# Low key parts of the attention scores on 64 rows of TensorE, two heads in turn, and the first scores among the values

## The chip, the core and the metric

The kernel runs on one core of a Trainium2 chip, in one launch. The metric is the device time of that launch in microseconds (us). Below, PE is the matrix engine (TensorE), PEld its weight loads, DVE VectorE, ACT ScalarE, POOL GpSimd, SP the engine that issues the transfers (DMA).

## What is computed

A decoder trunk of two layers on 256 positions of width 1024: a recurrent block with a squared-ReLU MLP, then sparse attention with a squared-ReLU MLP, each behind an RMS norm, and a last norm. The change touches the attention, of which this is the core (with 256 positions every block is selected and the window holds all earlier positions, so the selected and the window branch are plain causal attention with keys of their own):

```python
for each query block of 128 and each group of 4 heads:
    s_c = q.k_c - slope*d    # 15 compressed keys
    s_s = q.k_s - slope*d    # "selected" keys
    s_w = q.k_w - slope*d    # "window" keys
    o   = g0*softmax(s_c).v_c + g1*softmax(s_s).v_s + g2*softmax(s_w).v_w
```

There are 16 heads of 64 dimensions in 4 groups; a group shares its keys and values.

## The kernel before, in words

All of the large products are made in three passes of a reduced-precision float (fp32r): an operand x is split into a high part and a low part (x minus the high part), and PE adds high times high, high times low and low times high into one PSUM bank (`mm3`, L317 to L320). Weights come by DMA in pieces of 128 by 1024, ACT or DVE writes the high part (L326), DVE the low part (L323), in the order of `weight_pieces`. PE's program therefore is a long row of matmuls of 256 columns, lines L318, L319 and L320.

The attention section is recorded as tasks (`add`) with an engine, an assumed duration, what they read and write, and a due time. `Plan.emit` then lays the tasks out with these durations and a random seed (`SEEDS`), and the instructions of each engine are written in that order. Nothing is reordered on the chip afterwards: each engine works through its own row and waits on semaphores.

The steps of the section:

- `cproj` and `kchunk` (0, 0 and 0, 1) make the compressed inputs and the keys of the first two groups; `hidden` (L955), `kc_out` (L965) and `vc_out` (L984) make the compressed keys and values. `hidden` and the later `pv` (L1162) address 64 columns of PE's array at a time, two such halves in turn; `kc_out` and `vc_out` address 64 rows; every other matmul uses all 128 rows and 128 columns.
- `values` (L1005 to L1007) makes values and gates: 8 steps over the width, each with four matmul triples into four banks, and 96 matmuls in all.
- `qchunk(c)` makes the queries of two heads that lie in two groups. Its result sits in two tiles: `sa[c]` holds the high part of the first head's query in rows 0 to 63 and its low part in rows 64 to 127; `sb[c]` holds the second head's, high in rows 64 to 127, low in rows 0 to 63. The low parts get into the other rows by DMA (`move`).
- `kchunk(gp, br)` makes keys for two groups. `kh` has the high part of each group's keys twice, in both halves of the rows (the second copy by DMA); `kl` has the low part in the group's own rows, by DMA, and zeros in the other 64 rows (a POOL memset, L869).
- `scores(s)`: one head in three parts: both branches for the first 128 queries (288 columns with the compressed keys), the window or the selected branch for the last 128 queries (272 columns) and the other one (256 columns). Each part is two matmuls into one of three banks (2, 3, 4 in turn): L1098 with `kh` (all 128 rows, high and low query times high key) and L1099 with `kl` (all 128 rows, of which 64 of `kl` are zero). DVE then takes the bank (L1109 adds the distance term and takes the row's extreme, L1116 the same for the compressed keys, each followed by a short read of the accumulator), ACT takes the exponential (L1112).
- `rescale` (DVE, ACT), `transposes` (six on PE, L1147) and `pv` (probabilities times values, L1162) follow for each head or pair of heads. Probabilities lie in `pts`, of which there are NPT = 3, by head in turn.
- The fillers: between the parts of the scores PE does the remaining projections (`fillers`) and the first half of the output projection (`out_t`), all of them rows of L318 to L320.

The order before: `values` right after the compressed keys, then `qchunk(0)`, and the first scores at a due time of 37; the stages of the heads are TSTAGE = 5 apart.

Of the kernel before, what the change touches and what calls it, by code (L numbers as in the profile page):

```python
# [15 lines left out]
OP = mybir.AluOpType  # L16
# [15 lines left out]
NPT, NTL = 3, 3  # L32
TSTAGE, FPS = 5.0, 3.25
CST = (3.5, 7.5, 11.5, 15.2)
SEEDS, ROUNDS, SHIFT = (64, 5), 6, 1.5
# [16 lines left out]
def weight_pieces():  # L52

    order = []
    order += [{"c": ("in", 8 + i), "y": ("in", i)}[k] for k, i in RG_ORDER if k != "g"]
    order += [("out", m) for m in range(8)]
    order += mlp_pieces(0)
    order += [("ck", 0), ("ck", 1), ("cv", 0), ("cv", 1), ("ks", 0), ("kw", 0)]
    order += [("v", i) for i in range(4)]
    order += [("q", m) for m in range(4)]  # L60
    order += [("ks", 1), ("kw", 1)]
    order += [("q", m) for m in range(4, 8)]
    order += [("o0", m) for m in range(4)]
    order += [("o1", m) for m in range(4)]
    order += mlp_pieces(1)
    return order
# [153 lines left out]
def trunk_kernel(ctx: ExitStack, tc: tile.TileContext, x_in, vec_in, const_in, w2_in, wts, out):  # L220
# [607 lines left out]
    with ExitStack() as ph:  # L828
# [17 lines left out]
        kh, kl = (at.tile([P, 4 * GK + NCP], F32R, name=n) for n in ("kh", "kl"))  # L846
        kpair = lambda y, g, n: y[:, g * GK:g * GK + 2 * (S + NCP)].rearrange("p (b k) -> p b k", b=2)[:, :, :n]
        kcomp = lambda y: y[:, :4 * GK].rearrange("p (g k) -> p g k", g=4)[:, :, P:PC]
# [20 lines left out]
        add("pool", 1.74, lambda e: e.memset(kl.bitcast(F32), 0.0), w=["kl"], t=-9)  # L869
# [27 lines left out]
        def kchunk(gp, br, b, t, step):  # L897
            z, zk = proj_t(("ks", "kw")[br], gp, b, t, step)
            t += 4 * step
            x, xk, l_, lk = turn()  # L900
            add("dve", 0.34, lambda e: e.tensor_tensor(x, z(), rs, op=OP.mult), r=[zk, "rs"], w=[xk], t=t)
            x, l_ = two_blocks(x), two_blocks(l_)
            for hf in range(2):
                g = gp * 2 + hf
                add(HI, copy(kset(kh, g, br), x), r=[xk], w=[("k", g, br), ("k", g, br, 1)], t=t + 0.5)
            add("dve", 0.34, diff(l_, x, kset(kh, gp * 2, br)), r=[xk, ("k", gp * 2, br), ("k", gp * 2, br, 1)], w=[lk], t=t + 1)
            for hf in range(2):
                own, oth, g = own_(hf), own_(1 - hf), gp * 2 + hf
                move(kset(kh, g, br)[oth], kset(kh, g, br)[own], [("k", g, br)], [("k", g, br, 1)], t + 0.8)
                move(kset(kl, g, br)[own], l_[own], [lk, "kl"], [("k", g, br, 2)], t + 1.2)  # L910

        def kkeys(g, br):
            return [("k", g, br), ("k", g, br, 1), ("k", g, br, 2)]
# [49 lines left out]
        def kc_out(t):  # L963
# [4 lines left out]
            add("act", 0.1, lambda e: e.copy(kcomp(kh), o4()), r=[("ps", 6)], w=["kch"], t=t)  # L968
            for hf in range(2):
                own = own_(hf)  # L970
                add("dve", 0.15, lambda e, own=own, hf=hf: e.tensor_tensor(
                    kcomp(kl)[own, hf::2], o4()[own, hf::2], kcomp(kh)[own, hf::2].bitcast(F32), op=OP.subtract),
                    r=[("ps", 6), "kch", "kl"], w=[("kcl", hf)], t=t)
# [17 lines left out]
        def values(t):  # L991
            banks = ((2, 3), (4, 5))
            ncol = (S + 48, S)
            vz = [[zview(("v", h, b), banks[h][b], lambda x, b=b: x[:, :ncol[b]]) for b in range(2)] for h in range(2)]
            for i in range(4):
                wh, wl, wk = weight("v", i, t + 2.8 * i)
                for kk in range(2):
                    k = 2 * i + kk
                    for h in range(2):
                        def run(e, wh=wh, wl=wl, k=k, kk=kk, h=h):  # L1000
# [8 lines left out]
                            t=t + 2.8 * i + 1.4 * kk + 0.7 * h)  # L1009
            t += 11.2  # L1010
# [64 lines left out]
        def scores(s, t):  # L1075
            p, c, hf = heads[s]
            g = 2 * p + hf
            slope = float(2.0 ** (-8.0 * (g * 4 + c + 1) / 16))
            cc = (4 * p + c) % NQ
            x, xk = (sb, sa)[1 - hf][cc], ("sb" if hf else "sa", cc)  # L1080
            xk = [xk, xk + (1,)]
            mx, sm, pt = mxs[s % 4], sms[s % 4], pts[s % NPT]
            a, cj = s // 4, s % 4
            cview = lambda y, n, k: y[:, :2 * n].rearrange("p (b k) -> p b k", b=2)[:, :, :k]
            parts = ((0, lambda x: cview(x, PC, PC), lambda y: kpair(y, g, PC), (0, 1), 0.26),
                     (1, lambda x: x[:, :S + NCP], lambda y: y[:, g * GK:g * GK + S + NCP], (0,), 0.25),
                     (1, lambda x: x[:, :S], lambda y: y[:, g * GK + S + NCP:(g + 1) * GK], (1,), 0.23))
            for i, (qc, view, keys_, sets, d) in enumerate(parts):
                nk = (qc + 1) * P
                n = sn["n"]  # L1090
                sn["n"] += 1
                b = sbank[n % 3]
                bk = [("ps", b)]
                z = zview(("s", s, i), b, lambda x: x)

                def run(e, z=z, qc=qc, view=view, keys_=keys_):
                    qs = slice(qc * P, (qc + 1) * P)
                    e.matmul(view(z()), x[:, qs], keys_(kh), start=True, stop=False)  # L1098
                    e.matmul(view(z()), x[:, qs], keys_(kl), start=False, stop=True)  # L1099
                add("pe", d, run, r=xk + ["kl", "kch", ("kcl", 0), ("kcl", 1)] + kkeys(g, 0) + kkeys(g, 1), w=bk, t=t)  # L1100
                for b in sets:
                    o, j = qc * 2 * P + b * nk, 2 * qc + b
                    mk, pk = ("mx", s % 4, j), ("pt", s % NPT, qc, b)
                    row = pt[:, o:o + nk]
                    dist = cst[:, C_D0 + qc * P:C_D0 + qc * P + nk]
                    src = (lambda z, b=b: cview(z(), PC, P)[:, b]) if qc == 0 else (
                        (lambda z: z()[:, :S]) if b else lambda z: cview(z(), PC, P))
                    shape = two_blocks if (qc, b) == (1, 0) else lambda y: y
                    add("dve", (0.2, 0.34)[qc], lambda e, z=z, src=src, shape=shape, dist=dist, row=row, j=j: e.tensor_tensor_reduce(  # L1109
                        shape(row), src(z), shape(dist), -slope, -NEG, OP.add, OP.min, mx[:, j:j + 1]),  # L1110
                        r=bk + ["cst"], w=[mk, pk], t=t + 0.3)
                    add("act", (0.39, 0.49)[qc], lambda e, row=row, j=j: e.activation(  # L1112
                        row, row, AF.Exp, bias=mx[:, j:j + 1], scale=-1.0, accum_out=sm[:, j:j + 1]), r=[mk, "tab"],
                        w=[pk, ("sm", s % 4, j)], t=t + 0.6)
                if 0 in sets:
                    add("dve", 0.22, lambda e, z=z, qc=qc: e.tensor_tensor_reduce(  # L1116
                        css[a % 2][:, cj, qc], z()[:, P:PC], cst[:, C_DC + qc * NCP:C_DC + (qc + 1) * NCP], -slope, -NEG, OP.add,
                        OP.min, cmx[a % 2][:, 2 * cj + qc:2 * cj + qc + 1]),
                        r=bk + ["cst", ("sq", 0), ("sq", 1)], w=[("cs", a % 2), ("cm", a % 2)], t=t + 0.35)
# [91 lines left out]
        table(AF.Exp, 24)  # L1211
        values(20.5)
        gate_t(34)
        qchunk(0, 6, 34, PJ)
        T0, T = 37.0, TSTAGE
        fillers = [("q", c) for c in (1, 2, 3)] + [("ks", 1), ("kw", 1)] + [("q", c) for c in (4, 5, 6, 7)]
        step = T / FPS
        events = []
        for i, (nm, c) in enumerate(fillers):
            t = T0 + 4 * i * step  # L1220
# [4 lines left out]
        for m in range(8):  # L1225
            t = T0 + (n0 + 2 * m) * step
            events.append((t, 0, lambda m=m, t=t: out_t(0, m, (len(fillers) + m) % 2, t, step)))
        for s in range(16):
            events.append((T0 + s * T, 1, lambda s=s: scores(s, T0 + s * T)))
# [168 lines left out]
```

## Time and profile before

| | before |
|---|---|
| median of 3 runs | 570.66 us (570.56 to 570.67) |
| the profiled execution | 571.1 us |
| its span in the profile | 569.3 us |
| granted PE clock in it | 0.996 |
| PE busy, of the span | 560.9 us |
| DVE, ACT, POOL busy | 407.0, 342.7, 40.1 us |
| instructions | 12420 |

The page of the profile gives busy times by engine, a strip of 40 slices, and groups of instructions by line. A matmul's duration in it is the modelled time through a pipeline, so matmuls overlap; how fast PE works is read from the distance between starts in the timeline. A row of the timeline is: start in us, duration in us, engine, line, operation, destination and source, rows*columns of the array, shape, count. Equal instructions that follow each other are one row with their count.

### The profile page before, as it was taken

The page shows a single profiled execution, that of the slowest core. Times are in us where ns is not written, and L with a number is a line of the kernel's source. Part 1 is how long each engine was busy: PE and PEld are TensorE (multiplying, and loading weights), DVE is VectorE, ACT ScalarE, POOL GpSimd, SP SyncE. Part 2 cuts the span into 40 slices and gives each one's busy share as a digit, 9 for nine tenths or more (in the row PEclk, how much of TensorE's full clock was granted, in tenths as well). Part 3 has the DMA queues.
Part 4 walks back from the last instruction along what each step waited for, and adds up shares of the span by engine and source line. Part 5 has one row for each costly group of instructions (what it writes and reads, how often), then busy time and mean ns, then how long its engine had stood idle before and what let it go on. Part 6 is the DMA issues. An engine that isn't in the chain of part 4 may idle for free.

```text
span 569.3 us, 12420 instructions
## 1 busy us (share of the span) xinstructions
PE 560.9 (99%) x4906; PEld 553.7 (97%) x4906; DVE 407.0 (71%) x877; ACT 342.7 (60%) x666; POOL 40.1 (7%) x55
## 2 busy tenths in 40 slices
PE   9999999999999999999999999999999999999995
PEld 8989999999999999999999999999999999999995
DVE  6999989766775664565749999989867775553532
ACT  7799675865664443444456988886865664443410
POOL 1000000000000211221000000000000000222310
PEclk9999999999999999999999999999999999999998
DMA  8936468556657456456685232354676666566402
GB/s 318 407 98 209 121 214 255 184 189 191 195 194 235 155 204 222 163 190 221 212 264 154 65 114 57 112 171 144 198 230 193 191 202 231 156 205 218 126 1 74
DMA packets 33225, 103.66 MB, mean 182 GB/s; under 512 B 3856, under 2 KB 8080, under 8 KB 33168
## 3 DMA queue, kind: packets, MB, share of 16 engines
q1 hardware_dynamic: 32624, 102.42, 55.8%
q8 instruction: 38, 0.62, 0.4%
q10 hardware_dynamic: 544, 0.46, 0.2%
q14 instruction: 19, 0.16, 0.1%
HBM read 99.23 MB, written 1.05 MB: 176 GB/s over the span
## 4 chain that ended last, share of the span: by engine, by line
PE 95%; DVE 2%; issue 1%; DMA 1%; ACT 1%; DVEq 0%; POOL 0%; SPq 0%; ACTq 0%; POOLq 0%
PE bank L318 28%; PE bank L319 27%; PE bank L320 27%; PE bank L1162 3%; PE bank L686 2%; PE bank L1147 2%; PE bank L1098 1%; PE bank L1099 1%; PE bank L567 1%; DMA pt<-tt 1%; PE bank L1005 1%; DVE wlo L323 1%; PE bank L1006 1%; PE bank L1007 1%; ACT whi L326 1%
## 5 line engine op out<-in xcount | busy, mean ns | idle before, releaser
L318 PE MATMUL bank<-hhl,whi 128*128 128x256 f32 x768 | 213.2, 278 | 0.0
L319 PE MATMUL bank<-hhl,whi 128*128 128x256 f32 x768 | 212.4, 277 | 0.0
L320 PE MATMUL bank<-hhl,wlo 128*128 128x256 f32 x768 | 212.2, 276 | 0.0
L287 DVE TENSOR_TENSOR wlo<-raw,whi 128x1024 fp32r<-128x1024 f32 x115 | 143.2, 1266 | 1.9 <-ACT whi L278 1.9
L319 PEld LDWEIGHTS bank<-hhl,whi 128*128 128x128 f32 x768 | 144.3, 188 | 0.3 <-DVE hhl L576 0.2
L318 PEld LDWEIGHTS bank<-hhl,whi 128*128 128x128 f32 x768 | 144.3, 188 | 0.1
L320 PEld LDWEIGHTS bank<-hhl,wlo 128*128 128x128 f32 x768 | 144.2, 188 | 0.0
L318 PE MATMUL bank<-uhl,whi 128*128 128x256 f32 x512 | 141.5, 276 | 0.0
L319 PE MATMUL bank<-uhl,whi 128*128 128x256 f32 x512 | 141.4, 276 | 0.0
L320 PE MATMUL bank<-uhl,wlo 128*128 128x256 f32 x512 | 141.4, 276 | 0.0
L278 ACT CAST whi<-raw 128x1024 fp32r<-128x1024 f32 x116 | 118.1, 1039 | 23.1 <-issue 18.8
L318 PEld LDWEIGHTS bank<-uhl,whi 128*128 128x128 f32 x512 | 96.1, 188 | 0.0
L319 PEld LDWEIGHTS bank<-uhl,whi 128*128 128x128 f32 x512 | 96.1, 188 | 0.0
L320 PEld LDWEIGHTS bank<-uhl,wlo 128*128 128x128 f32 x512 | 96.1, 188 | 0.0
L323 DVE TENSOR_TENSOR wlo<-raw,whi 128x1024 fp32r<-128x1024 f32 (+2 forms) x72 | 77.4, 1091 | 7.0 <-ACT whi L326 6.9
L326 ACT CAST whi<-raw 128x1024 fp32r<-128x1024 f32 (+2 forms) x63 | 60.0, 966 | 21.4 <-PE bank L319 9.1
L522 DVE TENSOR_TENSOR xt<-xt,bank 128x256 f32<-128x256 f32 x39 | 15.9, 418 | 75.8 <-PE bank L320 75.8
L783 ACT ACTIVATE u<-t 128x256 f32<-128x256 f32 x64 | 26.7, 418 | 58.8 <-DVE t L778 58.6
L778 DVE SCALAR_TENSOR_TENSOR t<-bank,rstd 128x256 f32<-128x256 f32 x64 | 26.9, 423 | 39.7 <-PE bank L320 39.5
L1112 ACT ACTIVATE pt<-pt,mx 128x256 f32<-128x256 f32 (+1 forms) x64 | 28.7, 450 | 3.6 <-DVE mx L1109 3.2
L785 DVE TENSOR_TENSOR uhl<-u,uhl 128x256 fp32r<-128x256 f32 x64 | 26.6, 416 | 3.0 <-ACT uhl L784 3.0
L498 ACT ACTIVATE hhl<-xt,vec 128x256 fp32r<-128x256 f32 x8 | 4.1, 510 | 39.4 <-DVE xt L522 39.4
(201 smaller groups left out, 730.5 us busy)
## 6 DMA issues: line engine op xcount, KB each, us to landing
raw<-in_dram SPq DMA_DIRECT2D x171, 512.0 KB, 4.4
raw<-in_dram SPq DMA_DIRECT2D x4, 560.0 KB, 4.7
gw<-in_dram SPq DMA_DIRECT2D x4, 512.0 KB, 8.3
raw<-in_dram SPq DMA_DIRECT2D x6, 256.0 KB, 5.2
y<-in_dram SPq DMA_DIRECT2D x2, 512.0 KB, 6.8
pT<-in_dram SPq DMA_DIRECT2D x2, 512.0 KB, 5.7
xt<-in_dram SPq DMA_DIRECT2D x3, 256.0 KB, 5.2
kh<-kh SPq DMA_DIRECT2D x8, 64.0 KB, 2.8
```

The source lines that it names most:

```text
L278: (act.copy if eng is None else eng.tensor_copy)(hi_t[i % NSPL][:, :n], raw_of(i)[:, :n])
L287: (eng or dve).tensor_tensor(lo[:, :n], raw_of(i)[:, :n], hi[:, :n].bitcast(F32), op=OP.subtract)
L318: pe.matmul(ps, wh, xh, start=start, stop=False)
L319: pe.matmul(ps, wh, xl, start=False, stop=False)
L320: pe.matmul(ps, wl, xh, start=False, stop=stop)
L323: return lambda e: e.tensor_tensor(o, a, h.bitcast(F32), op=OP.subtract)
L326: return lambda e: (e.copy if e is act else e.tensor_copy)(o, a)
L778: dve.scalar_tensor_tensor(t, z, 0.0, rs, op0=OP.max, op1=OP.mult)
L783: act.activation(u, t, AF.Square)
L785: later(lambda: dve.tensor_tensor(ul[m], u, uh[m].bitcast(F32), op=OP.subtract))
L1112: add("act", (0.39, 0.49)[qc], lambda e, row=row, j=j: e.activation(row, row, AF.Exp, bias=mx[:, j:j + 1], scale=-1.0, accum_out=sm[:, j:j ...
L1162: two = lambda c, w, y, **k: [e.matmul(o()[own_(hf), c0 + c.start:c0 + c.stop], w(hf), y(hf), **k) for hf in range(2)]
```

## The change

**Scores.** `scores` now takes a pair of heads (the first from `sa`, the second from `sb`). Each of the three parts is four matmuls into two banks: both heads with `kh` on all 128 rows, then both heads with `kl`, the first on rows 0 to 63 and the second on rows 64 to 127. `kl` becomes half as wide: the low keys of a group lie in its own rows, with another group's in the rows that were zero. DVE writes them there itself, so the eight DMAs and the POOL memset for `kl` are gone. What DVE and ACT do with a bank is the same, in a function of its own (`taken`).

**Order.** The pieces of weights and the steps go: queries 0, first half of the values, queries 1, second half of the values, then the other fillers. The first scores are due at 25.5 (V0 + T1) instead of 37. The values use banks 4 to 7 instead of 2 to 5, and the first two pairs of scores use banks 2 and 3 alone, the later ones banks 2, 3 and 4 in turn. NPT is 4, FPS 3.5 (fillers for each stage) instead of 3.25, and the seed of the attention's plan is another one.

```diff
-NPT, NTL = 3, 3
-TSTAGE, FPS = 5.0, 3.25
+NPT, NTL = 4, 3
+TSTAGE, FPS = 5.0, 3.5
+V0, T1 = 20.5, 5.0
-SEEDS, ROUNDS, SHIFT = (64, 5), 6, 1.5
+SEEDS, ROUNDS, SHIFT = (64, 94), 6, 1.5
...
-    order += [("v", i) for i in range(4)]
-    order += [("q", m) for m in range(4)]
+    order += [("q", 0), ("v", 0), ("v", 1), ("q", 1), ("v", 2), ("v", 3), ("q", 2), ("q", 3)]
...
-        add("pool", 1.74, lambda e: e.memset(kl.bitcast(F32), 0.0), w=["kl"], t=-9)
...
-            add("dve", 0.34, diff(l_, x, kset(kh, gp * 2, br)), r=[xk, ("k", gp * 2, br), ("k", gp * 2, br, 1)], w=[lk], t=t + 1)
+            add("dve", 0.34, diff(kset(kl, gp, br), x, kset(kh, gp * 2, br)), r=[xk, ("k", gp * 2, br), ("k", gp * 2, br, 1)],
+                w=[("kl", gp, br)], t=t + 1)
...
-                move(kset(kl, g, br)[own], l_[own], [lk, "kl"], [("k", g, br, 2)], t + 1.2)
...
-        def values(t):
-            banks = ((2, 3), (4, 5))
+        def values(part, t):
+            banks = ((4, 5), (6, 7))
...
-                b = sbank[n % 3]
+                bs = [sbank[(sn["n"] + hf) % (3 if sp > 1 else 2)] for hf in range(2)]
...
-                    e.matmul(view(z()), x[:, qs], keys_(kh), start=True, stop=False)
-                    e.matmul(view(z()), x[:, qs], keys_(kl), start=False, stop=True)
-                add("pe", d, run, r=xk + ["kl", "kch", ("kcl", 0), ("kcl", 1)] + kkeys(g, 0) + kkeys(g, 1), w=bk, t=t)
+                    for hf in range(2):
+                        e.matmul(view(zs[hf]()), xs[hf][:, qs], keys_(kh, gs[hf]), start=True, stop=False)
+                    for hf in range(2):
+                        e.matmul(view(zs[hf]()), xs[hf][own_(hf), qs], keys_(kl, p)[own_(hf)], start=False, stop=True)
+                add("pe", d, run, r=xk, w=[("ps", b) for b in bs], t=t)
...
-        values(20.5)
-        gate_t(34)
-        qchunk(0, 6, 34, PJ)
-        T0, T = 37.0, TSTAGE
+        qchunk(0, 0, V0, PJ)
+        values(0, V0 + 2.7)
+        qchunk(1, 1, V0 + 8.3, PJ)
+        values(1, V0 + 11)
+        gate_t(V0 + 17)
+        T0, T, F0 = V0 + T1, TSTAGE, V0 + 17.0
```

Changed lines shift the numbers: the two score matmuls L1098 and L1099 become L1095 and L1097, DVE's L1109 and L1116 become L1116 and L1123, the values L1005 to L1007 become L1004 to L1006, the transposes L1147 become L1154, `pv` L1162 becomes L1169.

On PE, the first scores of the program, before: they follow the end of a projection (`bank_3726`), and one head (`sa`) does its three parts one after the other, each with `kh` and then `kl`.

```order
L320 MATMUL bank_3726<-hhl,wlo_92 128x256
L1098 MATMUL bank_3760<-kh,sa_3225 128x272
L1099 MATMUL bank_3760<-kl,sa_3225 128x272
L1098 MATMUL bank_3766<-kh,sa_3225 128x288
L1099 MATMUL bank_3766<-kl,sa_3225 128x288
L1098 MATMUL bank_3769<-kh,sa_3225 128x256
L1099 MATMUL bank_3769<-kl,sa_3225 128x256
L318 MATMUL bank_3773<-hhl,whi_86 128x256
```

The first scores now, in the midst of the values (L1004 to L1006): both heads of the pair do one part, `kh` and `kh`, then `kl` and `kl`, and the values go on.

```order
L1006 MATMUL bank_3567<-whi_88,hhl 128x256
L1095 MATMUL bank_3621<-kh,sa_3225 128x288
L1095 MATMUL bank_3623<-kh,sb_3229 128x288
L1097 MATMUL bank_3621<-kl,sa_3225 128x288
L1097 MATMUL bank_3623<-kl,sb_3229 128x288
L1004 MATMUL bank_3572<-whi_88,hhl 128x304
```

The two `kl` rows of a part use half of the array's rows each, and all rows around them use the whole array; the first scores moved from behind the values to the middle of them.

Further on, on PE, with bank numbers (bank2, bank3, bank4 are the banks of the scores), before: between two parts stand the transposes of an earlier head, and each part has a bank of its own.

```order
L1147 MATMUL bank6_3859<-cst_101,pt_3243 128x128 x3
L1098 MATMUL bank2_3870<-kh_3245,sa1_3226 128x288
L1099 MATMUL bank2_3870<-kl_3246,sa1_3226 128x288
L1098 MATMUL bank3_3874<-kh_3245,sa1_3226 128x272
L1099 MATMUL bank3_3874<-kl_3246,sa1_3226 128x272
L1098 MATMUL bank4_3881<-kh_3245,sb1_3230 128x256
L1099 MATMUL bank4_3881<-kl_3246,sb1_3230 128x256
```

Now, in the sixth pair: two parts with only the six transposes of another head between them, and the second part writes bank2 again, which the first one has filled.

```order
L1095 MATMUL bank2_4393<-kh_3245,sa1_3226 128x288
L1095 MATMUL bank3_4395<-kh_3245,sb1_3230 128x288
L1097 MATMUL bank2_4393<-kl_3246,sa1_3226 128x288
L1097 MATMUL bank3_4395<-kl_3246,sb1_3230 128x288
L1154 MATMUL bank5_4400<-cst_101,pt_3243 128x128 x3
L1154 MATMUL bank6_4404<-cst_101,pt_3243 128x128 x3
L1095 MATMUL bank4_4418<-kh_3245,sa1_3226 128x272
L1095 MATMUL bank2_4420<-kh_3245,sb1_3230 128x272
```

A part now holds two of the three banks, so that each part shares a bank with the one before it.

More of the change, by code (lines that the diff above doesn't have):

```diff
@@ L1073, in compressed, with scores @@
             add([("act", 0.3, 0.0), ("dve", 0.2, 0.15)], lambda e: copy(pc, ct_())(e), r=b7, w=[pk], t=t)
[L1075 to L1078, printed above, removed]
+        def scores(sp, t):
+            p, c, _ = heads[2 * sp]
             cc = (4 * p + c) % NQ
[L1080 to L1083, printed above, removed]
+            xs, gs = (sa[cc], sb[cc]), (2 * p, 2 * p + 1)
+            xk = [k for n in ("sa", "sb") for k in ((n, cc), (n, cc, 1))]
+            xk += ["kch", ("kcl", 0), ("kcl", 1)] + [k for g in gs for br in range(2) for k in kkeys(g, br)]
@@ new lines, in scores, with taken @@
+                add("pe", d, run, r=xk, w=[("ps", b) for b in bs], t=t)
+                for hf, z in enumerate(zs):
+                    taken(2 * sp + hf, z, [("ps", bs[hf])], qc, nk, sets, t)
+        def taken(s, z, bk, qc, nk, sets, t):
+            p, c, hf = heads[s]
+            slope = float(2.0 ** (-8.0 * ((2 * p + hf) * 4 + c + 1) / 16))
+            a, cj = s // 4, s % 4
+            mx, sm, pt = mxs[s % 4], sms[s % 4], pts[s % NPT]
+            cview = lambda y, n, k: y[:, :2 * n].rearrange("p (b k) -> p b k", b=2)[:, :, :k]
+            for b in sets:
+                o, j = qc * 2 * P + b * nk, 2 * qc + b
+                mk, pk = ("mx", s % 4, j), ("pt", s % NPT, qc, b)
+                row = pt[:, o:o + nk]
+                dist = cst[:, C_D0 + qc * P:C_D0 + qc * P + nk]
+                src = (lambda z, b=b: cview(z(), PC, P)[:, b]) if qc == 0 else (
+                    (lambda z: z()[:, :S]) if b else lambda z: cview(z(), PC, P))
+                shape = two_blocks if (qc, b) == (1, 0) else lambda y: y
+                add("dve", (0.2, 0.34)[qc], lambda e, src=src, shape=shape, dist=dist, row=row, j=j: e.tensor_tensor_reduce(
+                    shape(row), src(z), shape(dist), -slope, -NEG, OP.add, OP.min, mx[:, j:j + 1]),
+                    r=bk + ["cst"], w=[mk, pk], t=t + 0.3)
+                add("act", (0.39, 0.49)[qc], lambda e, row=row, j=j: e.activation(
+                    row, row, AF.Exp, bias=mx[:, j:j + 1], scale=-1.0, accum_out=sm[:, j:j + 1]), r=[mk, "tab"],
+                    w=[pk, ("sm", s % 4, j)], t=t + 0.6)
+            if 0 in sets:
+                add("dve", 0.22, lambda e: e.tensor_tensor_reduce(
+                    css[a % 2][:, cj, qc], z()[:, P:PC], cst[:, C_DC + qc * NCP:C_DC + (qc + 1) * NCP], -slope, -NEG, OP.add,
+                    OP.min, cmx[a % 2][:, 2 * cj + qc:2 * cj + qc + 1]),
+                    r=bk + ["cst", ("sq", 0), ("sq", 1)], w=[("cs", a % 2), ("cm", a % 2)], t=t + 0.35)
```

70 lines of the change are left out of this document (26 added, 44 removed).

## The prediction

> **What bounds the kernel now.** I read the page first. Its busy row for the engines, and the strip of the granted clock:
>
> ```profile
> PE 560.9 (99%) x4906; PEld 553.7 (97%) x4906; DVE 407.0 (71%) x877; ACT 342.7 (60%) x666; POOL 40.1 (7%) x55
> PEclk9999999999999999999999999999999999999998
> ```
>
> PE is busy for 560.9 of 569.3 us, at full clock. That is a mean over the stages, so I cut the attention into windows: before the compressed keys, the values and first queries, the scores, their end. Columns are PE, PEld, DVE, ACT and POOL in us with their counts, then clock and DMA.
>
> ```profile
> 284.00:305.00 21.00, 20.64 (x167) 20.25 (x167) 12.87 (x26) 10.44 (x17) 0.58 (x4) 1.00 0.73 228
> 305.00:360.00 55.00, 55.00 (x519) 52.63 (x519) 52.55 (x293) 49.40 (x164) 0.00 (x0) 1.00 0.30 92
> 360.00:378.00 18.00, 17.98 (x171) 16.53 (x167) 16.36 (x58) 14.66 (x39) 0.00 (x0) 1.00 0.36 110
> ```
>
> DVE is 61% busy among the values and 96% among the scores, and still PE is never without work there. The waits of PE from 266 to 380 us say the same; these two rows are the whole answer:
>
> ```profile
> PE bank L955 <- DMA pt<-tt: 0.4, 1, 0.4
> PE bank L965 <- ACT sq L959: 0.4, 1, 0.4
> ```
>
> So 0.8 us of waiting is all that a better order can win in this section; the load on DVE and ACT, which the earlier scores would spread, costs PE nothing today. What counts is the time that PE needs for its own row, and the program has as many matmuls after as before. I therefore sum on PE alone, against the profiled execution (571.1 us, span 569.3, so 1.8 around it); the median of the runs is 0.4 below it.
>
> **The pass with the low keys.** One head's scores in the timeline of PE (start, duration; two parts left out):
>
> ```profile
> 305.45 0.29 PE L1098 MATMUL bank<-kh,sa 128*128 128x272 f32 x1
> 305.57 0.29 PE L1099 MATMUL bank<-kl,sa 128*128 128x272 f32 x1
> 305.70 0.30 PE L1098 MATMUL bank<-kh,sa 128*128 128x288 f32 x1
> ...
> 306.21 0.28 PE L318 MATMUL bank<-hhl,whi 128*128 128x256 f32 x1
> ```
>
> Six matmuls from 305.45 to 306.21 are 0.76 us, 0.127 each, so the `kl` half of a head is 0.38 us. If the two heads of a pair run their `kl` passes at the same time, one of the two is saved: 8 pairs x 0.38 = 3.0 us, and I take 2.9, since the second starts a little later. The trace has no pair of row halves, but pairs of column halves, in `pv`:
>
> ```profile
> 323.96 0.28 PE L319 MATMUL bank<-hhl,whi 128*128 128x256 f32 x1
> 324.07 0.28 PE L320 MATMUL bank<-hhl,wlo 128*128 128x256 f32 x1
> 324.28 0.66 PE L1162 MATMUL bank<-pc,bd 128*64 128x128 f32 x8
> 324.76 1.47 PE L1162 MATMUL bank<-pT,vv 128*64 128x256 f32 x16
> ...
> 327.90 0.88 PE L1147 MATMUL bank<-cst,pt 128*128 128x128 f32 x6
> 328.53 0.37 PE L1098 MATMUL bank<-kh,sa 128*128 128x272 f32 x1
> ```
>
> Eight halves of 128 columns take 324.76 - 324.28 = 0.48 us, 0.06 each, where six transposes of the same length on the whole array take 0.63, 0.105 each: halves do run two at a time. The saving runs from 0 (halves of rows one after the other) to 3.0; the nearest row is this one, so 2.9.
>
> **The price of going to half the array and back.** The rows above show it too. L320 starts 0.11 after L319, but L1162 starts 0.21 after L320, and its first eight need 0.48 instead of 4 x 0.105 = 0.42: 0.10 + 0.06, so 0.16 us to go in. The way out, from another `pv`:
>
> ```profile
> 359.71 0.93 PE L1162 MATMUL bank<-pT,vv 128*64 128x128 f32 x10
> 360.57 0.39 PE L318 MATMUL bank<-oh,whi 128*128 128x256 f32 x1
> 360.79 0.28 PE L319 MATMUL bank<-ol,whi 128*128 128x256 f32 x1
> 360.91 0.28 PE L320 MATMUL bank<-oh,wlo 128*128 128x256 f32 x1
> ```
>
> The ten end at 360.64, and with the usual 0.27 of one the last began at 360.37. L318 follows 0.20 later instead of 0.10, and L319 0.22 after that instead of 0.12: 0.20 us to come out. These are halves of columns. For halves of rows the program has one stretch, `kc_out` and `vc_out`; on PE:
>
> ```profile
> 285.34 0.43 PE L965 MATMUL bank<-sq,w2raw 64*128 64x64 f32 x2 [0.36 <-ACT sq L959]
> 285.76 0.66 PE L984 MATMUL bank<-w2raw,sq 64*128 64x64 f32 x4
> 286.35 0.41 PE L1005 MATMUL bank<-whi,hhl 128*128 128x304 f32 x1
> 286.59 0.30 PE L1006 MATMUL bank<-wlo,hhl 128*128 128x304 f32 x1
> 286.73 0.30 PE L1007 MATMUL bank<-whi,hhl 128*128 128x304 f32 x1
> ```
>
> and its weight loads:
>
> ```profile
> 285.76 0.52 PEld L984 LDWEIGHTS bank<-w2raw,sq 64*128 64x128 f32 x4
> 286.34 0.19 PEld L1005 LDWEIGHTS bank<-whi,hhl 128*128 128x128 f32 x1
> 286.45 0.19 PEld L1006 LDWEIGHTS bank<-wlo,hhl 128*128 128x128 f32 x1
> ```
>
> Four loads of 0.19 within 0.52 start every 0.11, the last at 286.09. The next one, for the whole array, starts 0.25 later although its data were there (L1005 had used the same piece of weights before). Loads normally run under the matmul ahead of them; this one waited for that matmul to leave the array. So L1006 starts 0.24 after L1005 instead of the 0.14 from L1006 to L1007. Together 0.14 + 0.10 = 0.24, less some 0.05 for the slow start of L984 behind its own wait: about 0.2. It isn't the change from f32 to fp32r: where that happens on the whole array, the load keeps its step.
>
> ```profile
> 267.51 0.53 PEld L514 LDWEIGHTS bank<-ones,acc 128*128 128x128 f32 x4
> 267.96 0.19 PEld L318 LDWEIGHTS bank<-hhl,whi 128*128 128x128 f32 x1
> ```
>
> Four loads from 267.51 at 0.11 end at 267.95, and there L318 begins. The Trainium skill says the same in words ("TensorEngine Tiling (Array Packing)", Tiling Modes, Key Properties: changing the tiling mode, not just the tile, drains the engine) and gives no price; the trace agrees, with the 0.25 between two loads.
>
> After the change each of the 24 parts (8 pairs x 3) stands alone between matmuls of the whole array, as the order shows, so it goes in once and comes out once: 48 changes. Way out: 0.20, from the row halves themselves, not under 0.14 (the delay of the load alone). Way in: no row has it for row halves (L965 came in behind a wait for ACT); bounds 0 and 0.2, and I take 0.18, nearest the 0.16 of the column halves, whose loads are half as wide. Sum: 24 x (0.20 + 0.18) = 9.1 us.
>
> **Waits.** The order of the steps can win the 0.8 us above only if the place is filled better. In the new order `vc_out`, which needs one more copy than `kc_out`, stands first behind 12 matmuls of queries instead of 12 of values: I cost this at nothing, bounds -0.4 and +0.4. The first scores stand 42 matmuls of values (0.13 each, 5.4 us) behind the queries they use. Groups of DVE between 285 and 375 us (shape, count, busy us, mean ns of one), and a row of the transfers (median us to landing):
>
> ```profile
> L1109 DVE CUSTOM_DVE_ANT_0 pt<-bank,cst 128x256 f32<-128x256 f32 x32 | 13.2, 418 | 1.0 <-PE bank L1099 0.9
> L1109 DVE CUSTOM_DVE_ANT_0 pt<-bank,cst 128x128 f32<-128x128 f32 x32 | 8.7, 285 | 0.6 <-PE bank L1099 0.6
> L1116 DVE CUSTOM_DVE_ANT_0 sq<-bank,cst 128x16 f32<-128x16 f32 x32 | 5.3, 168 | 0.6 <-PE bank L1099 0.5
> L1109 DVE DVE_READ_ACCUMULATOR2_ANT mx<- 128x1 f32 x64 | 5.3, 83 | 0.0
> L1116 DVE DVE_READ_ACCUMULATOR2_ANT cm<- 128x1 f32 x32 | 2.7, 83 | 0.0
> L889 DVE SCALAR_TENSOR_TENSOR tt<-bank,cst,rstd 128x256 f32<-128x256 f32 x8 | 3.8, 481 | 0.6 <-PE bank L320 0.5
> L323 DVE TENSOR_TENSOR tl<-tt,sa 128x256 fp32r<-128x256 f32 x8 | 3.4, 421 | 0.0
> L326 DVE CAST sb<-tt 128x256 fp32r<-128x256 f32 x7 | 2.0, 288 | 0.0
> ```
>
> ```profile
> sb<-tl SPq DMA_DIRECT2D x8, 64.0 KB, 2.0
> ```
>
> The queries need 0.48 + a cast of 0.29 + 0.42 on DVE and two transfers, issued one behind the other, of 2.0 to landing: 3.2, and some 4.3 with the issue and DVE's queue. That fits under 5.4. A part's two banks are free again when DVE has taken both: for the first part 4 x (0.285 + 0.083) + 2 x (0.168 + 0.083) = 2.0 us, for the second 1.5, for the third 1.0. Between two parts PE mostly has 12 filler matmuls and often transposes (1.4 to 2.0 us), and sometimes the transposes alone (0.63), where the next part, which shares a bank, can wait 0.5 us. Before, a part held one bank of three and PE did not wait. I put 0.3 us on all these waits, bounds 0 and 1.5; what PE loses in the drains DVE gains as time to catch up. The DMAs, the memset and the DVE copies that go were hidden, since PE never waited for `kl`: nothing.
>
> **The sum.** -2.9 + 9.1 + 0.3 = +6.5 us: 577.6 for a profiled execution, 577.2 against the median of 570.66. By itself this case spans 48 x 0.14 - 3.0 = +3.7 to 48 x 0.20 - 2.9 + 1.5 = +8.2, so 574.4 to 578.9.
>
> **Rivals.**
> 1. *No price for row halves* (ends on the other side): PE lets weight loads for half the rows pass the running matmul and comes back without a drain. Then only the saving is left, 570.7 - 2.9 = 567.8. For it: within a mode the loads of L984 keep their 0.11, and no way in has been seen. Against it: the 0.25 at the way out. It decides as soon as a change costs less than 2.9 / 48 = 0.06 us. The Trainium skill leads there ("TensorE: Matmul & The Clock Gate", Part 3, span model: matmuls on different row groups take one matmul and some 4 ns for each further tile, with no term for the change); no run here shows it. Chance 0.14.
> 2. *Only the way out costs*: loads for half the rows start under the running matmul, since the stretch above shows the way out alone. 24 x 0.20 - 2.9 + 0.3 = +2.2: 572.9, from 571.5 to 574.4. Chance 0.12.
> 3. *The halves of rows run one after the other*: the drain stays, the saving goes: +9.1 + 0.3 = +9.4, 580.1. Against it: the pairs of column halves. Chance 0.04.
> 4. *Banks*: DVE, 96% busy, gives the banks back late, and each part waits 0.15 us more: 24 x 0.15 = 3.6 on top, 580.8. It decides where DVE's other work, a low part of weights for instance, stands between the two heads of a part. Against it: DVE had the same work before and PE never waited, and 8 us of idle time among the values take some of it now. Chance 0.04.
>
> **The numbers.** My forecast has 0.66. A measurement of this kernel can tell about 0.2%, 1.1 us, from no change. Faster: rival 1, 0.14. Within 0.2% (569.5 to 571.8): the low edge of rival 2, 0.03. Slower: the rest, 0.83. The range leaves out rival 1 and the far end of 4: from the low edge of rival 2, 571.5, to 580.5. The forecast's own range is 574.4 to 578.9.
>
> **What would show it.** In the timeline of the weight loads after: two loads of L1097 0.2 after the second L1095 instead of 0.12, starting together, and the next whole-array load 0.2 after them; a part of four matmuls takes 0.75 to 0.8 us from its first start to the next filler's second, where four in a row took 0.5. If the two L1097 start 0.12 apart, the halves don't overlap (rival 3); if L1097 follows L1095 in 0.12, rival 2 or 1 holds. Waits of PE for L1116 and L1123 of more than 1.5 us in the sum are rival 4. A time under 571.5 proves the price of the way out wrong.

## The result, and the profile after

| | before | after |
|---|---|---|
| median of the runs | 570.66 us (569.71 to 570.96, 5 runs) | 578.63 us (576.83 to 578.98, 5 runs) |
| the profiled execution | 571.1 us | 576.83 us |
| its span | 569.3 us | 575.0 us |
| PE busy, of the span | 560.9 us | 566.0 us |

The changed kernel takes 1.0131 times as long (95% interval 1.0110 to 1.0153; intervals stand in brackets from here on): 8.0 us more between the medians, where 6.5 were forecast. That is inside the forecast's own range of 574.4 to 578.9, at its upper end. In a second job it gave a median of 577.64 and a ratio of 1.0122 [1.0107, 1.0137]. (Two slow executions are left out of the numbers: one of `full_rows` at 948.9 us and a granted clock of 0.557, which was the profiled one, so that this kernel ran again as `full_rows_2`, and one of `full_rows_2` at 2010.4 us.)

The page of after, the same two rows as of before:

```profile
PE 566.0 (98%) x4906; PEld 552.5 (96%) x4906; DVE 406.4 (71%) x869; ACT 344.0 (60%) x674; POOL 39.2 (7%) x54
PEclk9999999999999999999999999999999999999998
```

The number of matmuls is the same, the clock is the same, and PE is as good as always busy: 5.1 us more of it. The windows of after over the values and the scores (PE, PEld, DVE, ACT, POOL, clock, DMA):

```profile
284.00:305.00 21.00, 20.75 (x161) 19.85 (x162) 13.08 (x43) 12.92 (x31) 0.00 (x0) 1.00 0.63 202
305.00:360.00 55.00, 54.33 (x461) 47.72 (x460) 47.64 (x243) 45.09 (x147) 1.53 (x4) 1.00 0.35 105
```

Between 305 and 360 us PE is busy for 54.33 of 55 us, but in this time it gets through 461 matmuls instead of 519, and loads weights for 47.7 us instead of 52.6. Not all of this is a loss, since the window no longer holds the same work. The fair comparison is the same order without row halves (`full_rows_2`, an experiment below):

```profile
305.00:360.00 55.00, 53.97 (x493) 51.92 (x492) 49.14 (x256) 48.09 (x156) 1.53 (x4) 1.00 0.35 114
```

It gets through 493, so 32 of the 58 go with the row halves. PE is as busy, yet slower, and the busy share doesn't tell: a matmul lasts 0.30 us in the timeline where the next one starts 0.13 later, so a step that grows to 0.23 leaves no gap. DVE went from 52.55 to 47.64 us in the same window, and now it is DVE that waits for the scores (10.7 us before the rows of 256 columns, where it was 1.0):

```profile
L1116 DVE CUSTOM_DVE_ANT_0 pt<-bank,cst 128x256 f32<-128x256 f32 x32 | 12.9, 422 | 10.7 <-PE bank L1097 10.6
```

All the waits of PE from 266 to 402 us:

```profile
PE bank L983 <- ACT sq L326: 0.6, 1, 0.6
PE bank L1169 <- DVE pc L326: 0.5, 1, 0.5
PE bank L1095 <- DVE mx L1116: 0.2, 1, 0.2
```

They are 1.3 us, after 0.8 before. So the waits explain 0.5 of the 5.7 us between the two spans. Most of the rest is in the parts themselves. The first part in the timeline of PE, among the values:

```profile
291.69 0.30 PE L1095 MATMUL bank<-kh,sa 128*128 128x288 f32 x1
291.82 0.30 PE L1095 MATMUL bank<-kh,sb 128*128 128x288 f32 x1
292.05 0.40 PE L1097 MATMUL bank<-kl,sa 64*128 64x288 f32 x1
292.05 0.40 PE L1097 MATMUL bank<-kl,sb 64*128 64x288 f32 x1
292.38 0.41 PE L1004 MATMUL bank<-whi,hhl 128*128 128x304 f32 x1
292.62 0.30 PE L1005 MATMUL bank<-wlo,hhl 128*128 128x304 f32 x1
292.76 0.30 PE L1006 MATMUL bank<-whi,hhl 128*128 128x304 f32 x1
```

and in that of the weight loads:

```profile
291.69 0.19 PEld L1095 LDWEIGHTS bank<-kh,sb 128*128 128x128 f32 x1
292.05 0.18 PEld L1097 LDWEIGHTS bank<-kl,sa 64*128 64x128 f32 x1 [0.17 <-issue]
292.05 0.18 PEld L1097 LDWEIGHTS bank<-kl,sb 64*128 64x128 f32 x1
292.38 0.19 PEld L1004 LDWEIGHTS bank<-whi,hhl 128*128 128x128 f32 x1
```

The two `kl` passes start together, as the change meant them to. But the first starts 0.23 us after the second `kh`, where whole-array neighbours are 0.13 apart. L1004 comes 0.33 later, and L1005 0.24 after that, where L1006 follows at the usual 0.14. The rows of the loads show where: the load of the second `kh` starts with the first `kh`, 0.13 ahead of its own matmul, as loads on the whole array do here; the loads for L1097 start only with their own matmuls (the load side stands idle for 0.17 us, and nothing that the profile shows holds it), and so does the load for L1004, which follows the pair.

### The profile page after: what moved, and what is told of

Same layout as the page of the kernel before. It is cut to its first block, busy times and chain, and to the rows that moved or that the text cites. A ratio compares the mean times of both kernels' runs of the same rounds, so it can differ in the third digit from the quotient of the medians.

```text
span 575.0 us, 12403 instructions
## 1 busy us (share of the span) xinstructions
PE 566.0 (98%) x4906; PEld 552.5 (96%) x4906; DVE 406.4 (71%) x869; ACT 344.0 (60%) x674; POOL 39.2 (7%) x54
## 4 chain that ended last, share of the span: by engine, by line
PE 95%; DVE 2%; DMA 1%; ACT 0%; issue 0%; SPq 0%; DVEq 0%; POOL 0%; ACTq 0%; POOLq 0%
PE bank L318 28%; PE bank L320 27%; PE bank L319 27%; PE bank L686 2%; PE bank L1169 2%; PE bank L1154 2%; PE bank L1097 1%; PE bank L1095 1%; PE bank L567 1%; PE bank L1004 1%; DMA pt<-tt 1%; PE bank L1005 1%; PE bank L1006 1%; DMA raw<-in_dram 1%; DVE wlo L323 1%; DVE xg L1292 0%
## 5 line engine op out<-in xcount | busy, mean ns | idle before, releaser
L318 PE MATMUL bank<-hhl,whi 128*128 128x256 f32 x768 | 214.5, 279 | 0.0
L319 PE MATMUL bank<-hhl,whi 128*128 128x256 f32 x768 | 212.4, 277 | 0.0
L318 PEld LDWEIGHTS bank<-hhl,whi 128*128 128x128 f32 x768 | 144.3, 188 | 1.6 <-issue 0.2
L319 PEld LDWEIGHTS bank<-hhl,whi 128*128 128x128 f32 x768 | 144.2, 188 | 0.1
L318 PE MATMUL bank<-uhl,whi 128*128 128x256 f32 x512 | 141.5, 276 | 0.0
L319 PE MATMUL bank<-uhl,whi 128*128 128x256 f32 x512 | 141.4, 276 | 0.0
L318 PEld LDWEIGHTS bank<-uhl,whi 128*128 128x128 f32 x512 | 96.1, 188 | 0.0
L319 PEld LDWEIGHTS bank<-uhl,whi 128*128 128x128 f32 x512 | 96.1, 188 | 0.0
L326 ACT CAST whi<-raw 128x1024 fp32r<-128x1024 f32 (+2 forms) x61 | 58.1, 965 | 19.8 <-PE bank L1006 6.0
L1119 ACT ACTIVATE pt<-pt,mx 128x128 f32<-128x128 f32 (+1 forms) x64 | 28.7, 452 | 2.7 <-DVE mx L1116 2.3
L1116 DVE CUSTOM_DVE_ANT_0 pt<-bank,cst 128x128 f32<-128x128 f32 (+1 forms) x64 | 21.3, 353 | 11.9 <-PE bank L1097 11.6
```

Of the source, the lines that this page charges most:

```text
L318: pe.matmul(ps, wh, xh, start=start, stop=False)
L319: pe.matmul(ps, wh, xl, start=False, stop=False)
L326: return lambda e: (e.copy if e is act else e.tensor_copy)(o, a)
L1116: add("dve", (0.2, 0.34)[qc], lambda e, src=src, shape=shape, dist=dist, row=row, j=j: e.tensor_tensor_reduce(shape(row), src(z), shape(di ...
```

## The experiments

**Row halves away, all else kept.** The low passes use all 128 rows again, one after the other. The row of PE's instructions is that of after, line by line.

```diff
-                        e.matmul(view(zs[hf]()), xs[hf][own_(hf), qs], keys_(kl, p)[own_(hf)], start=False, stop=True)
+                        e.matmul(view(zs[hf]()), xs[hf][:, qs], keys_(kl, p), start=False, stop=True)
```

> The changed kernel in its own order, but the pass with the low keys uses all 128 rows again for both heads (the other 64 rows add low query times another group's low key, of the size of rounding). So there is no going to half the array and back, and no saving. Theory (48 changes of about 0.19 us, less 2.9 us saved, make the change slower): 6.5 us less than the changed kernel, 570 to 572.5 us. Rival (the new order, its banks and DVE's work make it slower; the halves of rows cost nothing and save 2.9 us): the saving is lost and the time rises by about 2.9 us, to 579.5 or more.

Measured: 572.72 us, ratio 1.0029 [1.0019, 1.0040], 0.2 over the range expected and far from the rival's 579.5. It ran once more for its trace:

> full_rows once more, for a profile at full clock. It was 1.7 us over the kernel before, with all rows of the array in use. Both theories on these 1.7 us: the same time again, 572 to 572.8 us. In its timeline no load of weights should wait for a change of the array's shape at the scores, so a part takes 0.5 us.

Measured: 572.3 us, ratio 1.0030 [1.0017, 1.0042], span 571.5. The first part in its timeline, from the second `kh` on:

```profile
294.09 0.30 PE L1095 MATMUL bank<-kh,sb 128*128 128x288 f32 x1
294.23 0.30 PE L1097 MATMUL bank<-kl,sa 128*128 128x288 f32 x1
294.36 0.30 PE L1097 MATMUL bank<-kl,sb 128*128 128x288 f32 x1
294.50 0.30 PE L1004 MATMUL bank<-whi,hhl 128*128 128x304 f32 x1
294.63 0.30 PE L1005 MATMUL bank<-wlo,hhl 128*128 128x304 f32 x1
```

From the second `kh` to the second filler it takes 0.54 us with one pass more, against 0.80 in after: a part with row halves loses 0.26 us. The same in the 15 parts that projections follow (L318, L319): from the first `kh` to the second filler 0.946 us in after and 0.670 here (medians), so some 0.27 each. The parts ahead of transposes lose about 0.22, and the one that runs straight into a `pv`, itself on half of the array's columns, 0.06. Over the 24 parts that is 5.9 us. The medians say 578.63 - 572.72 = 5.9 and 577.64 - 572.30 = 5.3. What stays, 1.6 to 2.0 us over before, is not from the row halves. The waits of PE in this trace:

```profile
PE bank L954 <- DVE kl L323: 1.3, 1, 1.3
PE bank L983 <- ACT sq L326: 0.7, 1, 0.7
PE bank L1169 <- DVE pc L326: 0.6, 1, 0.6
PE bank L1095 <- DVE mx L1116: 0.4, 1, 0.4
```

3.0 us, 2.2 more than before, and the span is 2.2 us longer than before's: in this execution the waits are the whole remainder. The largest, 1.3 us of `hidden` (L954), lies ahead of the attention's scores and is in neither trace of after; before waits there for 0.4.

**Row halves in a third of the parts.** Only the part for the first 128 queries uses them: 16 changes instead of 48.

```diff
-                        e.matmul(view(zs[hf]()), xs[hf][own_(hf), qs], keys_(kl, p)[own_(hf)], start=False, stop=True)
+                        o = own_(hf) if len(sets) == 2 else slice(0, P)
+                        e.matmul(view(zs[hf]()), xs[hf][o, qs], keys_(kl, p)[o], start=False, stop=True)
```

> As full_rows, but the first of each pair's three parts (288 columns) has its low keys on row halves: 16 changes instead of 48. Theory: a third of the price and of the saving, so full_rows + (9.1 - 2.9) / 3 = full_rows + 2.1 us. If the halves cost nothing: full_rows - 1 us. If what costs is not the changes but the first one after a long stretch, or nothing that goes with their number: not a third.

Measured: 574.41 us, ratio 1.0063 [1.0048, 1.0078]: 1.7 us over `full_rows` of the same job. A third of 5.9 is 2.0. With intervals of 0.6 and 0.9 us to each side that fits, and its trace says the same more sharply: from the first `kh` to the second filler the first part takes 0.93 us, as in after, and the second one 0.62, as in `full_rows_2`. The cost lies in the parts that use row halves.

**No overlap, the same changes.** The second head's low pass also runs on rows 0 to 63, so it reads the first head's half (other numbers, the same work).

```diff
-                        e.matmul(view(zs[hf]()), xs[hf][own_(hf), qs], keys_(kl, p)[own_(hf)], start=False, stop=True)
+                        e.matmul(view(zs[hf]()), xs[hf][own_(0), qs], keys_(kl, p)[own_(0)], start=False, stop=True)
```

> The changed kernel, but the second head's low pass uses rows 0 to 63 like the first's, so that the two can't run at the same time (it leaves out the second head's low-key term and adds a term of low parts in its place). Theory (the two halves did overlap): 2.9 us more than the changed kernel, and the two matmuls start 0.12 us apart instead of together. Rival (they never overlapped): the same time as the changed kernel.

Measured: 579.89 us, ratio 1.0163 [1.0150, 1.0176]: 1.3 us over the median of after in its first job, 2.3 over that in its second, not 2.9. Its interval touches that of after in the first job and lies above that in the second. The trace is clearer than the times:

```profile
293.53 0.30 PE L1095 MATMUL bank<-kh,sb 128*128 128x288 f32 x1
293.76 0.40 PE L1097 MATMUL bank<-kl,sa 64*128 64x288 f32 x1
294.00 0.28 PE L1097 MATMUL bank<-kl,sb 64*128 64x288 f32 x1
294.21 0.41 PE L1004 MATMUL bank<-whi,hhl 128*128 128x304 f32 x1
294.46 0.31 PE L1005 MATMUL bank<-wlo,hhl 128*128 128x304 f32 x1
```

From the second `kh` to the second filler it is 0.93, against 0.80 in after, and in the same 15 parts 1.060 against 0.946: 0.11 to 0.13 us a part, 24 x 0.12 = 2.9 us. So the overlap is worth what was forecast; the times of after, which vary by 2 us, show only part of it. The two halves start 0.24 apart, not 0.12 as expected. With the halves one behind the other one can also see how a change divides: the four steps are 0.23, 0.24, 0.21 and 0.25 instead of 0.13 or 0.14. Each change adds 0.10 ahead of the first matmul in the new mode and 0.10 behind it; where the two halves start together, as in after, the second 0.10 of the way in and the first of the way out lie in the one step of 0.33.

**Each part changes twice.** `kh`, `kl`, `kh`, `kl` instead of both `kh` and then both `kl`: 96 changes, and nothing overlaps.

```diff
                     for hf in range(2):
                         e.matmul(view(zs[hf]()), xs[hf][:, qs], keys_(kh, gs[hf]), start=True, stop=False)
-                    for hf in range(2):
                         e.matmul(view(zs[hf]()), xs[hf][own_(hf), qs], keys_(kl, p)[own_(hf)], start=False, stop=True)
```

> The changed kernel with the four matmuls of a part in another order: first head on the whole array, its half, second head on the whole array, its half. 96 changes instead of 48, and no two halves side by side. Theory: 24 more ways in and out at 0.38 us, and the saving of 2.9 us gone: 12 us more than the changed kernel, about 589 us. If only the way out costs 0.2 us: 4.8 + 2.9 = 7.7 us more. If the changes cost nothing: 2.9 us more.

Measured: 589.57 us, ratio 1.0339 [1.0322, 1.0357], 9.7 us over `same_rows` in the same job, which has the same matmuls and half the changes: 9.7 / 48 = 0.20 us for one change. Its timeline shows them one by one:

```profile
292.47 0.29 PE L1095 MATMUL bank<-kh,sa 128*128 128x288 f32 x1
292.69 0.39 PE L1096 MATMUL bank<-kl,sa 64*128 64x288 f32 x1
293.02 0.40 PE L1095 MATMUL bank<-kh,sb 128*128 128x288 f32 x1
293.34 0.39 PE L1096 MATMUL bank<-kl,sb 64*128 64x288 f32 x1
293.67 0.41 PE L1004 MATMUL bank<-whi,hhl 128*128 128x304 f32 x1
293.91 0.31 PE L1005 MATMUL bank<-wlo,hhl 128*128 128x304 f32 x1
```

Five steps from 292.47 to 293.91 take 1.44 us where five whole-array steps take 5 x 0.13 = 0.65. Four changes: 0.79 / 4 = 0.20 each, the same as by the times.

**Where the other 1.6 to 2.0 us come from.** Two kernels take the pairs apart again. The first has the order of after, but single heads with one bank for each part, on all rows:

```diff
-                bs = [sbank[(sn["n"] + hf) % (3 if sp > 1 else 2)] for hf in range(2)]
+                b = sbank[sn["n"] % (3 if s > 3 else 2)]
...
-                    for hf in range(2):
-                        e.matmul(view(zs[hf]()), xs[hf][:, qs], keys_(kh, gs[hf]), start=True, stop=False)
-                    for hf in range(2):
-                        e.matmul(view(zs[hf]()), xs[hf][own_(hf), qs], keys_(kl, p)[own_(hf)], start=False, stop=True)
+                    e.matmul(view(z()), x[:, qs], keys_(kh, g), start=True, stop=False)
+                    e.matmul(view(z()), x[:, qs], keys_(kl, p), start=False, stop=True)
```

> The order of steps of the changed kernel (queries 0 ahead of the values, first scores among the values), but each head does its three parts by itself with one bank each, all rows in use, as before. Theory A (the 1.7 us that full_rows loses come from the order of the steps): 572 to 573 us. Theory B (they come from the pairs, which hold two of three banks): as the kernel before, 570 to 571 us.

Measured: 572.43 us (570.69 to 573.02), ratio 1.0026 [1.0014, 1.0038], the same as `full_rows`. So with the early scores the pairs cost nothing that these times can tell. But its profiled execution (571.05 us) shows only this wait:

```profile
PE bank L1094 <- DMA sa<-tl: 0.2, 1, 0.2
```

Its span of 569.2 us is that of before. The 1.7 us are in other executions than the one with a trace. The second kernel has before's order, seed and single heads, and only `kl` is new: half as wide, written by DVE, without the DMAs and the memset.

```diff
-        add("pool", 1.74, lambda e: e.memset(kl.bitcast(F32), 0.0), w=["kl"], t=-9)
...
-                move(kset(kl, g, br)[own], l_[own], [lk, "kl"], [("k", g, br, 2)], t + 1.2)
```

> The order of steps, the seed and the single heads of the kernel before, and only this of the change: low keys written by DVE straight into half as wide a tile, all 128 rows used (the other rows add low query times another group's low key), no DMAs and no memset for them. Both theories (PE never waited for the low keys, so what made them was hidden): as the kernel before, within 0.2%. Rival: the transfers for the low keys stood in SP's row ahead of those that the compressed keys wait for, and 0.4 us at most come off.

Measured: 570.74 us, ratio 1.0002 [0.9993, 1.0011]. The DMAs, the memset and the copies were hidden, as the prediction had it. So the remainder comes with the early order and what goes with it in `early_singles` (the seed 94, NPT, FPS, the banks of the values); these weren't tried apart. On the changed kernel's spread there is another run of it:

> The changed kernel once more, beside the one above on the same chip, for a second profile: its five runs lay at 576.8 and at 578.6 to 579.0 us. If the price of the changes explains the loss, both kinds of runs show the same 24 ways in and out (0.22 and 0.32 us between starts at the scores), and what differs by 2 us lies elsewhere, in a wait.

Measured: 577.64 us (577.26 to 578.36), span 575.5; its waits are the three of the first trace, 1.1 us in all, and its steps at the scores are those expected (medians of 0.22 on the way in, 0.32 on the way out). `hidden` waited 0 here, 1.3 in `full_rows_2`, 0.5 in `same_rows` and `twice`, 0.3 in `one_part`, with the same row of instructions ahead of it. In the order of before it varies too: 0.4 in before, 0.5 in `late_singles`, 0 in `late_pairs`. A wait that comes and goes by up to 1.3 us would fit the spread between runs; since only profiled executions have a trace, this isn't shown.

The traces allow a comparison without it: from the first matmul behind `hidden` to the first one behind the last `pv` every kernel has the same 856 matmuls. Before takes 94.98 us for them (283.16 to 378.14 in its timeline), `late_singles` 95.12, `early_singles` 95.57, `full_rows_2` 96.26, after 101.97 and 101.91, `same_rows` 104.52, `twice` 113.61. So in the traces the row halves cost 5.7 us, the lost overlap 2.6, a change (9.09 / 48) 0.19, and the early order 0.6 with single heads and 1.3 with pairs, less than the medians give it.

**Pairs without the early scores.** Before's order and seed 5, pairs with two banks for each part, all rows; then the same with row halves.

```diff
-NPT, NTL = 3, 3
+NPT, NTL = 4, 3
...
+                bs = [sbank[(sn["n"] + hf) % 3] for hf in range(2)]
...
+                        e.matmul(view(zs[hf]()), xs[hf][:, qs], keys_(kl, p), start=False, stop=True)
```

> The order of steps of the kernel before (values first, first scores due at 37), but heads in pairs with two banks for a part, all rows in use. Theory A (order): as the kernel before, 570 to 571 us. Theory B (pairs): 572 to 573 us.

Measured: 576.01 us, ratio 1.0091 [1.0074, 1.0108]. Both theories had said 573 at most: a miss for both. Waits of PE, and windows of 2 us where they lie:

```profile
PE bank L1095 <- DVE cm L1060: 1.0, 1, 1.0
PE bank L1154 <- DVE pt L1144: 0.8, 1, 0.8
PE bank L1073 <- DVE sq L1061: 0.4, 1, 0.4
PE bank L1154 <- ACT pT L326: 0.2, 1, 0.2
```

```profile
338.00:340.00 2.00, 1.04 (x7) 0.65 (x6) 1.96 (x14) 2.00 (x7) 0.00 (x0) 1.00 0.00 0
340.00:342.00 2.00, 1.01 (x7) 0.84 (x8) 2.00 (x17) 1.93 (x8) 0.00 (x0) 1.00 0.01 4
342.00:344.00 2.00, 2.00 (x11) 2.00 (x12) 2.00 (x10) 1.23 (x7) 0.00 (x0) 0.56 0.05 10
344.00:346.00 2.00, 1.93 (x9) 1.46 (x8) 1.25 (x7) 1.88 (x7) 0.00 (x0) 0.59 0.86 252
```

DVE is full and PE half idle from 338 to 342 us, and then the granted clock (third column from the end) is 0.56 and 0.59 for 4 us. The waits are 2.4 us, 1.6 more than before; the slower clock loses 2 x 0.44 + 2 x 0.41 = 1.7 us more; some 1.8 of the 5.1 us between the spans stay unassigned. The drop of the clock isn't needed for the loss: the three other executions have a mean granted clock of 0.996 to 0.997, like before, against 0.994 in this one, and take as long (575.7 to 576.2 us).

> late_pairs with the low keys of the two heads on row halves: the change without its early scores. Theory (48 changes at 0.18 to 0.19 us, less 2.9 saved): late_pairs + 5.8 to 6.5 us. Rival (the early scores make the price, by leaving the parts alone among the values): clearly less than 5.

Measured: 582.25 us (580.2 to 584.2), ratio 1.0201 [1.0168, 1.0234], 6.2 us over `late_pairs`. That is in the range expected, but not cleanly: in its profiled execution (584.2 us) the clock was down for longer.

```profile
344.00:346.00 2.00, 1.05 (x4) 0.60 (x4) 2.00 (x12) 2.00 (x10) 0.00 (x0) 0.69 0.02 4
346.00:348.00 2.00, 2.00 (x11) 1.85 (x9) 1.09 (x10) 0.54 (x4) 0.00 (x0) 0.50 0.44 88
...
354.00:356.00 2.00, 2.00 (x24) 1.58 (x20) 0.00 (x0) 0.00 (x0) 0.00 (x0) 0.75 0.27 66
```

At 0.50 from 346 to 354, that is 2 x 0.31 + 8 x 0.50 + 2 x 0.25 = 5.1 us lost, 3.4 more than in `late_pairs`; the spans differ by 8.0, so 4.6 are left for the row halves. The four executions say the same: two have a mean granted clock of 0.989 and take 583.7 and 584.2 us, two have 0.998 and take 580.2 and 580.8, which is 4.0 to 5.1 over those of `late_pairs`. So the 6.2 between the medians holds some clock. Since one order of tasks may be bad by chance, both ran again with the changed kernel's seed:

```diff
-SEEDS, ROUNDS, SHIFT = (64, 5), 6, 1.5
+SEEDS, ROUNDS, SHIFT = (64, 94), 6, 1.5
```

> The order of before with pairs of heads, all 128 rows, as in the run late_pairs, with the seed 94 of the changed kernel for the order of the attention's tasks instead of 5. Theory B (pairs that start late are short of banks and of DVE, whatever the order): waits of PE of over 2 us and stretches of the scores at a granted clock well below 1 again, at least 574 us. Rival (one bad order): waits of at most 1.5 us, clock 1.00 throughout the scores, at most 572.7 us.

Measured: 579.47 us, ratio 1.0166 [1.0149, 1.0183]. The rival of one bad order falls: this one is worse still. The longest of its waits, and one window:

```profile
PE bank L1154 <- DVE pT L326: 1.2, 1, 1.2
PE bank L1095 <- DVE mx L1116: 1.0, 2, 0.7
PE bank L1095 <- DVE cm L1123: 0.9, 1, 0.9
PE bank L1154 <- DVE pt L1144: 0.9, 1, 0.9
```

```profile
344.00:348.00 4.00, 4.00 (x29) 3.48 (x29) 3.61 (x21) 3.30 (x15) 0.00 (x0) 0.57 0.14 33
```

With the two shorter ones of 0.6 its waits are 5.2 us, five of the six for DVE, and the clock drops in the same place. So pairs that start late wait for DVE in both orders tried. That the banks are what is short, rather than DVE's time, wasn't tried apart.

> The same with the low passes on row halves. By the starts of the 24 parts in the traces so far, row halves cost 5.9 us net (0.28 us for a part between fillers, 0.22 before transposes). Theory A (the price belongs to the parts and to nothing else): late_pairs_94 + 5.9, between 5.2 and 6.8, if the granted clock falls in neither or alike in both. Rival (the price depends on the order): a difference outside of 4.5 to 7.5 that the clock doesn't account for.

Measured: 584.67 us, ratio 1.0246 [1.0229, 1.0264], 5.2 us over `late_pairs_94`, the lower edge of what was expected, at about the same mean clock (0.990 to 0.992 against 0.991 to 0.994). In both late orders the parts that projections follow, where PE doesn't wait, lose 0.25 to 0.28 us by the starts, as in the early one. By the times the row halves so cost 4.0 to 5.2 us in the late orders, 5.3 and 5.9 in the early one.

## Why the prediction was right, and where it was off

- **What bounds the kernel.** Right. PE's own row sets the end. The earlier scores freed DVE (47.64 instead of 52.55 us in 305 to 360, and 49.14 in `full_rows_2`) and won nothing by that, since PE had not waited for it.
- **The saved passes, -2.9.** Right. The halves start together, and `same_rows` shows 0.11 to 0.13 us a part for it by the starts, 2.9 in all; by the stretch behind `hidden` it is 2.6, by the medians 1.3 to 2.3.
- **The price of a change, 0.20 out and 0.18 in, +9.1.** Right. `twice` against `same_rows` gives 0.20 for one; the parts of after against those of `full_rows_2` give a net 5.9, with the saving 8.8, so 8.8 / 48 = 0.18. The way in, which no row of before had, costs as much as the way out: 0.10 ahead of the first `kl` and 0.10 behind it, by the steps of `same_rows`. The Trainium skill's statement ("TensorEngine Tiling (Array Packing)", Tiling Modes, Key Properties) that changing the mode drains the engine agrees with this, and the cost is there in both directions. What the rows show is the delay of loads and matmuls; that the array empties meanwhile is the Trainium skill's account of it. The number of changes is 47 by the timeline, since one part runs straight into a `pv`; that moves the sum by 0.2 us. In its signs the prediction counted one step too few: it gave 0.75 to 0.8 us against 0.5 from a part's first start to the next filler's second, where in `full_rows_2` five steps, 0.67, lie between these starts and in after it is 0.93. The difference was right.
- **Rival 1, no price.** Fell. It gave 567.8 us; measured 578.63. It went with the span model of the Trainium skill ("TensorE: Matmul & The Clock Gate", Part 3, Measured speedup vs the span model). The part of that model on the pair itself, some 4 ns for each further tile, agrees with the trace: the two starts lie 3 to 4 ns apart in all 24 parts. The entry and the exit, which it has no term for, are three times the saving.
- **Rivals 2 and 3.** Fell, by the 0.23 on the way in and by the common start of the halves.
- **Rival 4, banks.** Fell here: waits of L1095 for DVE are 0.2 us, and DVE waits for PE instead. What it describes did happen once the early scores were taken away (`late_pairs`, `late_pairs_94`), so among the orders tried only the early one, with its settings, keeps the pairs from costing much. The prediction's reason against it, that DVE had the same work before and PE never waited, was not the right one: in the late order DVE also has the same work, and PE waits.
- **Waits, +0.3 with bounds 0 and 1.5.** Too small. This is the step that failed in size: with the row halves away, the early order still costs 1.6 to 2.0 us by the medians. In the trace of `full_rows_2` it is `vc_out` behind `sq` (0.7), the compressed `pv` behind `pc` (0.6), a bank (0.4), and `hidden` (1.3), a step that the prediction had not looked at since its own instructions don't change. The first three, less `kc_out`'s 0.4, are the 1.3 us by which the stretch behind `hidden` is longer than before's; `hidden` itself waits in both orders, by changing amounts, and can't be laid to the early one. `vc_out` first, costed at nothing, is a wait of 0.4 to 0.7 in every one of the early traces with pairs, in place of `kc_out`'s 0.4; it waits as long in the two late traces with seed 94 and not in `early_singles`, so it isn't a mark of the early scores alone. Where the rest lies in executions without a trace stays open.
- **Sum.** 5.9 for the row halves and 1.6 to 2.0 for the order make 7.5 to 7.9; measured 7.05 and 8.0. The forecast of 6.5 is short by the waits. Without the row halves the change still is no gain: none of the kernels tried was faster than before.

## What to carry to other kernels

Count the entries into a half-array mode and the exits, not the matmuls in it: here each cost 0.2 us, a matmul and a half, and a pair of halves saves one matmul, so by these numbers a stretch must save over 0.40 us, more than three such pairs side by side, before it gains anything (no run here has so long a stretch). Moving work forward to relieve an engine pays only if the engine that sets the end has waited for it; the list of waits says that before the work is done. And where a bound is taken for waits, look also at the steps ahead of the moved ones, whose own code doesn't change.

## What the runs showed that was not expected

- Short stretches of idle PE close to each other went ahead of a lower granted clock in all four traces of pairs in the late order. In `late_pairs`, gaps of 1.1 and 1.4 us between starts within 4 us are followed by 0.50 for the 3.3 us from 342.3 to 345.6 (the windows of 2 us above mix this with full clock); in `late_halves` it is 10 us. Other executions of the same two kernels have a mean clock of 0.996 to 0.998, and in `full_rows_2` gaps of 1.6 and 0.9 us, 5 us apart, left it at 1.00, so such gaps don't always do it. The Trainium skill's "TensorE: Matmul & The Clock Gate" (Why this matters for your kernels) asks for idle gaps below some 3 us; here no single gap was half as long as that, and the clock fell all the same. That page also tells of short idle times between groups that did so in another kernel (A second HAM failure mode: psum-queue depth-cycling), which is nearer to this.
- A change costs on both sides of the first matmul in the new mode, 0.10 us each (`same_rows`, `twice`). Who measures only the step into the mode sees half of it.
- A busy share can stay where it was while the work gets slower: with row halves PE is busy for 98.8% of 305 to 360 us with 461 matmuls, without them (`full_rows_2`) for 98.1% with 493.
